# Maximum over the last axis of 64 MiB: larger and fewer loads, a larger share for GpSimd, and VectorE's steps in a written order

## The chip, the cores and the metric

One core of one Trainium2 chip. The metric is the device time of one execution in microseconds (us); a kernel's time is the median of its executions. Each execution also has a **span**, from the first to the last instruction that the profiler records; the time is the span and some 1.8 us outside it. All runs of this study were in the fast state. VectorE is DVE in the profile, GpSimd is POOL, ScalarE is ACT, SyncE is SP, TensorE is PE (its weight loads PEld).

## The reference

```python
# x: float32 [32, 512, 1024], normally distributed
def reference(x):
    return np.max(x, axis=-1).astype(np.float32)
```

There are 16384 rows of 1024 numbers. Each of the 128 partitions gets 128 rows; below, "a row" is one row on every partition, 128 x 4 KiB. 64 MiB are read once and 64 KiB written.

## The kernel before

SyncE issues the loads into a ring of 46 rows. VectorE reduces most rows directly. For some late rows GpSimd helps with the first few blocks of 128 columns: TensorE transposes a block, ScalarE copies it from PSUM, GpSimd takes the maximum over the partitions, TensorE transposes the result back into a column ("back"), and VectorE merges it with what it reduced itself. The last two rows come in three pieces. Cuts are marked with `# ...`.

```python
BLOCKS = [
    [15, 15, 15, 14, 12, 11, 9, 8, 7, 6],
    [4, 3, 2, 2, 1, 1, 1],
]
RING = 46
SHARED = {7: (2, 3), 9: (4, 4), 11: (3, 3), 13: (2, 3), 16: (1, 1)}   # load: (rows, blocks of 128 columns)
# ...
    for sizes in BLOCKS:
        S = sum(sizes) + 2 * (sizes is BLOCKS[-1])
        xb = xf[first * P:(first + S) * P, :].rearrange("(p i) d -> p i d", p=P)   # S rows per partition
# ...
    def turn(j, c):                      # one chunk: transposes, copy, all-reduce
        # ...
                in_turn("PE", nc.tensor.transpose(
                    out=ps[:, k * P:(k + 1) * P],
                    in_=rows(j)[:, loads[j][1] - m + r + i, c0 * P:(c0 + 1) * P],
                    identity=ident,
                ))
        in_turn("ACT", nc.scalar.copy(out=sb[:, :W], in_=ps[:, :W]))
        in_turn("POOL", nc.gpsimd.partition_all_reduce(
            top[:, :W], sb[:, :W], P, bass_isa.ReduceOp.max))
    def back(j, c):                      # one transpose for each block again
        # ...
                in_turn("PE", nc.tensor.transpose(
                    out=share(j)[:, c0, r + i:r + i + 1],
                    in_=tops[j, c][0:1, k * P:(k + 1) * P],
                    identity=ident[0:1, 0:1],
                ))
# ...
    for p, q in ((0, 48), (48, 96), (96, P)):
        store = nc.scalar.dma_start(out=views[0][0][p:q], in_=views[0][1][p:q])
    nc.scalar.dma_start(out=views[1][0], in_=views[1][1])
```

A point to keep in mind: the row numbers of a block are split so that partition p has S rows next to each other. Neighbouring partitions therefore read memory S x 4 KiB apart, here 448 KiB in the first block (112 rows) and 64 KiB in the second (16 rows).

## Time and profile before

| | before |
|---|---|
| time, median (range of 4 executions beside the changed kernel) | 164.03 us (163.90 to 164.27) |
| span of the profiled execution | 162.3 us |
| bytes loaded, mean rate over the span | 67.11 MB, 414 GB/s |
| VectorE busy | 135.4 us |
| GpSimd's all-reduces | 7, 16.0 us |
| TensorE transposes | 76, two instructions each |

The lines of the profile and how they are read are in the prediction below: the load queue is busy to the end, and VectorE's queue ends just behind it.

### The profile page before, as it was taken

Reading aid. Unit: us, or ns where it says so; the run is one execution under the profiler, and the core shown is the slowest. Engines: PE = TensorE matmul, PEld = TensorE weight load, DVE = VectorE, ACT = ScalarE, POOL = GpSimd, SP = SyncE. Lnnn points to the kernel's source line nnn. Section 1 sums busy time; section 2 is a strip of 40 time slices with the busy share of each in tenths; the row PEclk is TensorE's granted clock in tenths of the full one; section 3 lists DMA queues with packets and bytes.
Section 4 is the critical chain, followed back from the end, with each engine's and each line's share of the span. In section 5 each row is a group of like instructions: output and inputs, shape, how many; then the busy total and the mean of one; then the engine's idle time right before and its main releaser. Section 6 shows DMA issues by size and latency. Waiting matters only on the chain.

```text
span 162.3 us, 305 instructions
## 1 busy us (share of the span) xinstructions
PE 14.0 (9%) x76; PEld 12.0 (7%) x76; DVE 135.4 (83%) x35; ACT 6.3 (4%) x8; POOL 16.2 (10%) x11
## 2 busy tenths in 40 slices
PE   0000000000000000000000000000003010736540
PEld 0000000000000000000000000000002010725440
DVE  3000079995999779998999999999999999999994
ACT  3000000000000000000000000000001000222020
POOL 0000000000000000000000000000000500095970
DMA  7999699988999699999998998999999999999990
GB/s 242 485 485 454 273 485 485 485 379 348 485 485 485 285 410 452 452 452 388 497 472 371 433 455 355 436 436 420 509 396 445 452 395 396 440 411 423 405 379 18
DMA packets 3200, 67.18 MB, mean 414 GB/s; under 512 B 640, under 2 KB 640, under 8 KB 1408
## 3 DMA queue, kind: packets, MB, share of 16 engines
q1 hardware_dynamic: 2880, 67.11, 96.7%
q10 hardware_dynamic: 320, 0.07, 0.2%
HBM read 67.11 MB, written 0.07 MB: 414 GB/s over the span
## 4 chain that ended last, share of the span: by engine, by line
DVE 57%; DMA 36%; issue 5%; DVEq 0%
DVE res L168 52%; DMA ring<-in_x_dram 36%; DVE fetched L168 5%; DVEq L249 0%
## 5 line engine op out<-in xcount | busy, mean ns | idle before, releaser
L168 DVE TENSOR_REDUCE res<-ring 128x15 f32<-128x15360 f32 (+10 forms) x15 | 124.1, 8302 | 23.7 <-DMA ring<-in_x_dram 23.7
L143 POOL PARTITION_ALL_REDUCE top<-sb x7 | 16.0, 2330 | 141.8 <-ACT sb L141 141.8
L135 PE MATMUL ps<-ident,ring 128*128 128x128 f32 x38 | 9.3, 425 | 133.8 <-DMA ring<-in_x_dram 133.8
L135 PEld LDWEIGHTS ps<-ident,ring 128*128 128x128 f32 x38 | 7.5, 223 | 134.1 <-issue 127.8
L141 ACT COPY sb<-ps 128x768 f32<-128x768 f32 (+3 forms) x7 | 5.1, 739 | 150.2 <-PE ps L135 150.2
L168 DVE TENSOR_REDUCE fetched<-ring 128x2 f32<-128x1280 f32 (+3 forms) x5 | 8.5, 1699 | 0.0
L161 PE MATMUL fetched<-ident,top 1*128 1x1 f32 x38 | 4.8, 243 | 10.8 <-DVE fetched L168 7.3
L161 PEld LDWEIGHTS fetched<-ident,top 1*128 1x128 f32 x38 | 4.5, 213 | 12.5 <-issue 8.0
L168 DVE TENSOR_REDUCE res<-res 128x2 f32<-128x672 f32 (+1 forms) x2 | 1.7, 858 | 0.0
L141 ACT ACT_TABLE_LOAD x1 | 1.3, 1283 | 0.7 <-PEq L238 0.7
L83 DVE MEMSET ident<- 128x128 f32 x1 | 0.2, 165 | 0.8 <-PEq L238 0.8
L168 DVE TENSOR_REDUCE res<-fetched 128x2 f32<-128x8 f32 (+3 forms) x5 | 0.7, 158 | 0.0
L90 DVE TENSOR_SCALAR rowno<-rowno 32x1 f32<-32x1 f32 x3 | 0.4, 146 | 0.1
L85 DVE TENSOR_TENSOR_SCAN colno<-ident 128x128 f32<-128x128 f32 x1 | 0.4, 425 | 0.0
L92 DVE TENSOR_SCALAR ident<-colno,rowno 128x128 f32<-128x128 f32 x1 | 0.3, 285 | 0.0
L87 DVE STREAM_TRANSPOSE rowno<-colno 128x32 f32<-128x32 f32 x1 | 0.2, 213 | 0.0
L238 POOL MEMSET const-float32-0.0<- 128x1 f32 x1 | 0.1, 98 | 0.2 <-issue 0.2
L238 POOL MEMSET const-bfloat16-1.0<- 128x1 bf16 x1 | 0.1, 101 | 0.0
L238 POOL MEMSET const-uint8-127<- 128x1 uint8 x1 | 0.1, 101 | 0.0
L238 POOL MEMSET const-float32-1.0<- 128x1 f32 x1 | 0.1, 99 | 0.0
L84 DVE MEMSET rowno<- 128x32 f32 x1 | 0.1, 85 | 0.0
## 6 DMA issues: line engine op xcount, KB each, us to landing
ring<-in_x_dram SPq DMA_DIRECT2D x3, 7680.0 KB, 38.4
ring<-in_x_dram SPq DMA_DIRECT2D x1, 7168.0 KB, 37.0
ring<-in_x_dram SPq DMA_DIRECT2D x1, 6144.0 KB, 33.4
ring<-in_x_dram SPq DMA_DIRECT2D x1, 5632.0 KB, 28.6
ring<-in_x_dram SPq DMA_DIRECT2D x1, 4608.0 KB, 39.1
ring<-in_x_dram SPq DMA_DIRECT2D x1, 4096.0 KB, 33.3
ring<-in_x_dram SPq DMA_DIRECT2D x1, 3584.0 KB, 29.0
ring<-in_x_dram SPq DMA_DIRECT2D x1, 3072.0 KB, 35.9
```

What stands on the lines that cost most here:

```text
L83: in_turn("DVE", nc.vector.memset(ident, 1.0))
L84: in_turn("DVE", nc.vector.memset(rowno, 0.0))
L85: in_turn("DVE", nc.vector.tensor_tensor_scan(out=colno, data0=ident, data1=ident, initial=-1.0, op0=ALU.add, op1=ALU.mult))
L87: in_turn("DVE", nc.vector.transpose(out=rowno, in_=colno[:, :32]))
L90: in_turn("DVE", nc.vector.tensor_scalar(out=part, in0=part, scalar1=float(q * 32), scalar2=None, op0=ALU.add))
L92: in_turn("DVE", nc.vector.tensor_scalar(out=ident, in0=colno, scalar1=rowno[:, 0:1], scalar2=None, op0=ALU.is_equal))
L135: in_turn("PE", nc.tensor.transpose(out=ps[:, k * P:(k + 1) * P], in_=rows(j)[:, loads[j][1] - m + r + i, c0 * P:(c0 + 1) * P], identity=i ...
L141: in_turn("ACT", nc.scalar.copy(out=sb[:, :W], in_=ps[:, :W]))
L143: in_turn("POOL", nc.gpsimd.partition_all_reduce(top[:, :W], sb[:, :W], P, bass_isa.ReduceOp.max))
L161: in_turn("PE", nc.tensor.transpose(out=share(j)[:, c0, r + i:r + i + 1], in_=tops[j, c][0:1, k * P:(k + 1) * P], identity=ident[0:1, 0:1],))
L168: return in_turn("DVE", nc.vector.reduce_max(out=out, in_=in_, axis=X))
L238: nc = _bacc.Bacc("TRN2", target_bir_lowering=False, num_devices=1)
```

## The change

Its intent: fewer loads (15 and three pieces instead of 17 and three), a ring fuller by one row, much more of the work for GpSimd (99 blocks instead of 38) and less for VectorE, and the steps of VectorE written in the order in which their inputs are expected. The result moves into the ring's tile. Cut to its core:

```diff
 BLOCKS = [
-    [15, 15, 15, 14, 12, 11, 9, 8, 7, 6],
-    [4, 3, 2, 2, 1, 1, 1],
+    [16, 15, 16, 15, 16, 15, 10, 7],
+    [5, 3, 3, 2, 1, 1, 1],
 ]
-RING = 46
-SHARED = {7: (2, 3), 9: (4, 4), 11: (3, 3), 13: (2, 3), 16: (1, 1)}
+RING = 47
+SHARED = {3: (4, 3), 5: (6, 5), 6: (10, 2), 7: (7, 1), 8: (3, 3), 9: (2, 4), 10: (2, 3), 11: (2, 3), 14: (1, 1)}
+PIECES = [(689, 335), (336, 688)]
+PLAN = """
+    d0 d1 d2 d3 t0 t1 b0 b1 p3 m3 d4 d5 t2 t3 t4 t5 b2 t6 b3 t7 b4 p5 b5 p6 t8 t9 t10 b6 b7
+    m5 p7 t11 b8 b9 b10 t12 m6 d8 t13 b11 p8 t14 m7 d9 b12 p9 b13 m8 d10 t15 p10 t16 p11 d12
+    b14 d13 b15 m9 m10 p14 t17 f0 b16 f1 b17 m11 m14 f2
+""".split()
@@
-    ring = once.tile([P, RING, D], F32)
-    res = once.tile([P, MID + D - W], F32)
+    ring = once.tile([P, I + RING * D], F32)
+    res = ring[:, :I]
@@
+    for step in PLAN:
+        issue()                       # each load whose slot has no reader left
+        kind, k = step[0], int(step[1:])
+        if kind in "dp":              # d: direct rows, p: the rest of shared rows
+            (direct if kind == "d" else partial)(k)
+            readers[k] -= 1
+        elif kind == "t":             # t: transposes, copy, all-reduce of a chunk
+            turn(k)
+            readers[chunks[k][0]] -= 1
+        elif kind == "b":             # b: a chunk's transposes back
+            back(k)
+        elif kind == "m":             # m: merge on VectorE
+            merge(k)
+        else:                         # f: the three pieces
+            inst = maximum(*tail[k])
# ... (the old loops and lists that this replaces are cut)
```

It also moves the border between the two blocks from row 112 to row 110, which at first looks like book-keeping: neighbouring partitions now read 440 and 72 KiB apart, and the last store writes 18 numbers (72 B) for each partition instead of 16 (64 B).

> **What bounds the kernel now.** I began with the page's engine shares, slices and queues.
>
> ```profile
> PE 14.0 (9%) x76; PEld 12.0 (7%) x76; DVE 135.4 (83%) x35; ACT 6.3 (4%) x8; POOL 16.2 (10%) x11
> ...
> DVE  3000079995999779998999999999999999999994
> ...
> q1 hardware_dynamic: 2880, 67.11, 96.7%
> ...
> DVE res L168 52%; DMA ring<-in_x_dram 36%; DVE fetched L168 5%; DVEq L249 0%
> ...
> res<-in_x_dram SPq DMA_DIRECT2D x1, 344.0 KB, 11.5
> ```
>
> The load queue is busy for 96.7% of the span. VectorE (DVE) is at 83%, but its low digits are all in the first 19 slices; the chain names both. To see which of the two sets the end I read VectorE's timeline, first and last part.
>
> ```profile
> 21.42 16.15 DVE L168 TENSOR_REDUCE res<-ring 128x15 f32<-128x15360 f32 x1 [18.91 <-DMA ring<-in_x_dram]
> 39.55 16.15 DVE L168 TENSOR_REDUCE res<-ring 128x15 f32<-128x15360 f32 x1 [1.98 <-DMA ring<-in_x_dram]
> ...
> 74.64 55.86 DVE L168 TENSOR_REDUCE res<-ring 128x14 f32<-128x14336 f32 x5 [0.79 <-DMA ring<-in_x_dram]
> ...
> 139.41 2.27 DVE L168 TENSOR_REDUCE res<-ring 128x2 f32<-128x2048 f32 x1
> ...
> 157.34 0.86 DVE L168 TENSOR_REDUCE res<-ring 128x1 f32<-128x689 f32 x1
> 158.24 0.85 DVE L168 TENSOR_REDUCE res<-res 128x2 f32<-128x672 f32 x1
> 159.01 0.22 DVE L168 TENSOR_REDUCE res<-fetched 128x2 f32<-128x8 f32 x2
> 159.15 0.86 DVE L168 TENSOR_REDUCE res<-res 128x1 f32<-128x689 f32 x1
> ```
>
> From 74.64 us on VectorE has no idle gap. Yet its end is no later than the data allow: the last piece is issued at 147.52 (below) and lands 11.5 us later (last line of the first fence), at 159.0, and its reduction starts at 159.15. So the kernel is **balanced**: the load stream ends at 159.0 and VectorE's queue ends within 0.15 us of it. Then come 0.86 us of reduction, the last store (1.4 us) and the close, to a span of 162.3; the timed median, 163.97, is 1.67 above the span.
>
> The stream's rate follows from the queue's timeline. From the ninth load on, an issue waits for the load eight places earlier, so these starts mark the landings of the loads of 7, 6, 4 and 3 rows:
>
> ```profile
> 131.63 0.33 SPq L185 DMA_DIRECT2D ring<-in_x_dram  x1
> 138.93 0.33 SPq L204 DMA_DIRECT2D ring<-in_x_dram  x1
> 143.82 0.33 SPq L206 DMA_DIRECT2D res<-in_x_dram  x1
> 147.52 0.33 SPq L207 DMA_DIRECT2D res<-in_x_dram  x1
> ```
>
> Six rows took 7.30 us, four 4.89, three 3.70, and fifteen 39.55 - 21.42 = 18.13. From 15 and 4: (18.13 - 4.89)/11 = 1.204 us for a row and **0.07 us for each load** besides. Six rows give 7.29: the stream never starves.
>
> [...] A row of 128 x 4 KiB in 1.204 us is 435.5 GB/s[...]. [...] From 16.15 us for 15 rows and 2.27 for 2 a row costs 1.067 us (0.96 elements per ns) and an instruction about 0.14, of which some 0.08 lie under its neighbour. [...] Two rows take 2.27 us at 139.41 with GpSimd idle and 2.28 at 150.23 with it busy[...]. This matters, since GpSimd will work far longer.
>
> **The change, part by part.**
>
> *Fewer loads.* 17 whole loads become 15 (16, 15, 16, 15, 16, 15, 10, 7, 5, 3, 3, 2, 1, 1, 1), with the same three pieces. Same bytes, two times 0.07 us less: the last piece lands at 159.0 - 0.14 = 158.85. For that the queue must never run dry. A ring of 47 rows holds 16+15+16. By the rule above the loads land at 22.6, 40.7, 60.1, 78.2, 97.6, 115.7, 127.8, 136.3, 142.4, 146.1, 149.8, 152.3, 153.5, 154.8 and 156.1. The nearest thing to a late issue is the load of 7, which waits for VectorE to finish the fifth load (97.6 + 17.2 = 114.8) and is due at 127.8. Hidden, with 13 us to spare.
>
> *Less work for VectorE.* GpSimd takes 38 blocks of 128x128 before and, counted from the list (12+30+20+7+9+8+6+6+1), 99 after. 61 blocks are 61/8 rows x 1.067 = 8.1 us less reduction. But the new work is beside loads that come in fatter and later pieces, so it shows as idle time in front of loads 0 to 4, not at the end. What counts is VectorE's queue after its last wait for data. I laid it out with the durations above: it is idle for some 0.3 us before the load of 7 (136.3), then has 18.4 row-equivalents up to the last whole load, 1.33 more in two pieces, in 13 instructions, and seven merges at about 0.08: 19.7 x 1.067 + 13 x 0.065 + 0.6 = 22.4 us, plus some 0.2 for waits on its own last write. The third piece's reduction can start at 136.3 + 22.6 = 158.9 to 159.0. The data are there at 158.85. So again both ends meet: **159.0 against 159.15, 0.15 us won.** Both starts of the chain (first load one row larger, 1.2 us later) cost nothing, as the stream does not wait for VectorE.
>
> *More for TensorE, ScalarE, GpSimd.* The seven all-reduces show
>
> ```profile
> 142.07 3.22 POOL L143 PARTITION_ALL_REDUCE top<-sb  x1 [13.89 <-ACT sb L141]
> ...
> 150.13 2.50 POOL L143 PARTITION_ALL_REDUCE top<-sb  x1 [1.64 <-ACT sb L141]
> ```
>
> for 8 and 6 blocks: about 0.34 us a block and 0.5 fixed. 18 of them with 99 blocks: 18 x 0.5 + 99 x 0.34 = 43 us, all between 115.7 and 158 save two early ones: GpSimd becomes nearly full there. With transposes at 0.21 us a block, copies of 0.16 + 0.10 a block and returns at 0.107 a block, I stepped through the four engines with the waits of the built program. Each merge on VectorE must find its returns done: 142.2 against 142.9 for the load of 10, 145.4 against 147.3 for that of 7, 149.4 against 149.7 for that of 5, 154.6 and 155.4 against 156.0 for the next two, 158.1 and 158.3 against 158.85 for the last two. All in time, two of them by less than 0.7 us.
>
> *Order of steps and the tail.* The pieces now land in the ring and need the load of 10 read (about 136); they are due at 156. The stores are as before.
>
> The sum: -0.15 us, 163.97 to 163.8. As every margin errs on one side, I take 163.9.
>
> **The rivals.** *GpSimd becomes the bound.* For: margins of 0.3 and 0.7 us, and one chain of four engines with two buffers each. Against: the trace's durations repeat to 3%. With all-reduces 6% longer my layout loses 0.15 us, at 10% 1.0 us, at 20% 4 us (168.0). *The stream's rate changes.* Rows of 64 KiB per partition (16 rows) have not run in this trace; 48 rows are loaded so, and 1% in their rate is 0.6 us either way. The partition pitch in memory goes from 448 to 440 KiB and from 64 to 72 KiB. Nothing shows a dependence: the 4-row load of the second block has the same cost per row as the first. *VectorE was the true bound, and 8 us less work gives a gain.* Against: the last piece's landing at 159.0 forbids more than 0.15 us. *A load is issued late* by a wait the scheduler added: the waits that I read name only the readers of the slots overwritten.
>
> **Range and chances.** The stream's end is certain to some 0.2 us if rates hold; slips of GpSimd add 0 to 1. I take 163.4 to 164.8. A 2% gain (160.7) would need the stream 3 us shorter[...]: 0.01. A 2% loss (167.2) needs GpSimd 18% slower or a starved queue: 0.02.
>
> **What would show it.** Right: VectorE idle before each of loads 0 to 5, hardly after 136; spacing of 19.3 us for 16 rows; POOL near 42 us busy; the last reduction starting near 159.0. Wrong: VectorE idle with a TensorE or GpSimd releaser before a merge (first rival); 16-row spacing off 19.3 (second); a gap in the queue's busy share after slice 5 (fourth).

## The result

The changed kernel takes **165.73 us** (165.44 to 165.84, 4 executions) against 164.03: a ratio of 1.0100 (95% interval 1.0088 to 1.0113). A ratio here is the record's, over the fast runs of both kernels, so not quite the ratio of the quoted medians. The record notes no wrong result. The profiled execution has a span of 163.5 us, against 162.3; the four executions have 2.14 to 2.24 us outside the span, where the kernel before had 1.7 to 1.8. So of 1.7 us, 1.2 are inside the span and **about 0.4 outside it**.

The changed kernel's page, the lines that answer to the first fence of the prediction (engines; queues; chain):

```profile
PE 34.9 (21%) x198; PEld 30.1 (18%) x198; DVE 128.0 (78%) x40; ACT 14.6 (9%) x19; POOL 41.8 (26%) x22
...
q1 hardware_dynamic: 2592, 67.11, 95.8%
...
q8 instruction: 1, 0.02, 0.0%
...
DMA ring<-in_x_dram 70%; DVE ring L74 23%; DVE got L74 2%; SPq L215 1%; DVEq L269 0%
```

The share of the load queue fell though it carries the same bytes. And there is a queue that the kernel before does not have: q8, one transfer of 0.02 MB of kind "instruction". The page calls its share 0.0%, which is the share of sixteen engines' span; it says nothing of what one of the sixteen was doing for others. VectorE's timeline of the changed kernel (start, duration, engine, line, operation; in brackets the idle time before and what ended it):

```profile
22.91 17.22 DVE L74 TENSOR_REDUCE ring<-ring 128x16 f32<-128x16384 f32 x1 [20.39 <-DMA ring<-in_x_dram]
41.02 16.15 DVE L74 TENSOR_REDUCE ring<-ring 128x15 f32<-128x15360 f32 x1 [0.90 <-DMA ring<-in_x_dram]
60.37 17.22 DVE L74 TENSOR_REDUCE ring<-ring 128x16 f32<-128x16384 f32 x1 [3.20 <-DMA ring<-in_x_dram]
...
116.02 9.75 DVE L74 TENSOR_REDUCE ring<-ring 128x9 f32<-128x9216 f32 x1 [0.93 <-DMA ring<-in_x_dram]
...
137.58 6.70 DVE L74 TENSOR_REDUCE got<-ring 128x7 f32<-128x6272 f32 x1 [1.19 <-DMA ring<-in_x_dram]
...
158.42 1.75 DVE L74 TENSOR_REDUCE ring<-ring 128x1 f32<-128x689 f32 x2
160.09 0.22 DVE L74 TENSOR_REDUCE ring<-got 128x2 f32<-128x8 f32 x2
160.23 0.86 DVE L74 TENSOR_REDUCE ring<-ring 128x1 f32<-128x689 f32 x1
```

The spacing of the landings is as foreseen (19.35 us for 16 rows: 60.37 - 41.02), but two of them are late. The first load lands at 22.9 instead of 22.6. The load of 7 rows lands at 137.56 instead of 136.3; from there all is late by about 1.1 us, and the last reduction starts at 160.23 instead of 159.0.

Was VectorE held up by GpSimd's chain, the first rival? The view of who waited for whom, the lines for VectorE in the changed kernel:

```profile
DVE ring L74 <- DMA ring<-in_x_dram: 30.9, 6, 20.4
...
DVE got L74 <- DMA ring<-in_x_dram: 1.2, 1, 1.2
```

Apart from 0.8 us at its first instruction, VectorE waited for loads only. No merge was late.

In the traces each load has 16 landings, and the page counts 16 DMA engines; I take each landing for the part of one engine, and what one engine moves for the load queue is called a DMA ring below (not the ring of rows that holds the data). In the kernel before, the first load's last ring is 0.51 us behind its first (20.88 to 21.39) and stays so to the end. In the changed kernel this spread is 0.90 us at the first load (21.98 to 22.88), 0.85 at the load of 10 rows, and then **1.79 at the load of 7** (135.77 to 137.56), which holds to the last whole load (1.78). The other fifteen land the load of 7 by 136.63, within 0.86 us: one ring lost time between 128.1 and 137.6 and never made it up. The q8 transfer lies in just that stretch: 16,384 B, from 132.41 us, for 1.03 us; the trace's only packet of the load of 7 that is long (1.56 us instead of 1.06) begins at 133.43, as the transfer ends (132.41 + 1.03). The trace doesn't name the ring of a packet, so that both used one ring is read from these times; the five traces with a fetch show it six times, to within 0.02 us. The reduction waits for the slowest ring: that lands at 137.56, and the reduction starts at 137.58.

### The profile page after: what moved, and what is told of

Same layout as the page of the kernel before. It is cut to its first block, busy times and chain, and to the rows that moved or that the text cites. A ratio compares the mean times of both kernels' runs of the same rounds, so it can differ in the third digit from the quotient of the medians.

```text
span 163.5 us, 606 instructions
## 1 busy us (share of the span) xinstructions
PE 34.9 (21%) x198; PEld 30.1 (18%) x198; DVE 128.0 (78%) x40; ACT 14.6 (9%) x19; POOL 41.8 (26%) x22
## 4 chain that ended last, share of the span: by engine, by line
DMA 70%; DVE 25%; issue 1%; SPq 1%; DVEq 0%
DMA ring<-in_x_dram 70%; DVE ring L74 23%; DVE got L74 2%; SPq L215 1%; DVEq L269 0%
## 5 line engine op out<-in xcount | busy, mean ns | idle before, releaser
L74 DVE TENSOR_REDUCE ring<-ring 128x1 f32<-128x1024 f32 (+7 forms) x14 | 99.1, 7082 | 30.9 <-DMA ring<-in_x_dram 30.9
L146 POOL PARTITION_ALL_REDUCE top<-sb x18 | 41.6, 2371 | 117.5 <-ACT sb L144 114.3
L138 PE MATMUL ps<-ident,ring 128*128 128x128 f32 x99 | 22.7, 410 | 114.3 <-DMA ring<-in_x_dram 113.0
L138 PEld LDWEIGHTS ps<-ident,ring 128*128 128x128 f32 x99 | 18.6, 216 | 115.5 <-DVE ring L74 78.6
L74 DVE TENSOR_REDUCE got<-ring 128x2 f32<-128x1280 f32 (+7 forms) x9 | 27.5, 3072 | 1.2 <-DMA ring<-in_x_dram 1.2
L144 ACT COPY sb<-ps 128x640 f32<-128x640 f32 (+6 forms) x18 | 13.3, 746 | 143.0 <-PE ps L138 127.3
L156 PE MATMUL got<-ident,top 1*128 1x1 f32 x99 | 12.7, 240 | 10.6 <-POOL top L146 7.5
L156 PEld LDWEIGHTS got<-ident,top 1*128 1x128 f32 x99 | 11.4, 206 | 14.2 <-POOL top L146 9.5
L74 DVE TENSOR_REDUCE ring<-got 128x2 f32<-128x8 f32 (+7 forms) x9 | 1.3, 165 | 0.0
```

The lines of the kernel that those rows point to most:

```text
L74: return in_turn("DVE", nc.vector.reduce_max(out=out, in_=in_, axis=X))
L138: in_turn("PE", nc.tensor.transpose(out=ps[:, w:w + P], in_=rows(j)[:, loads[j][1] - m + r + i, c * P:(c + 1) * P], identity=ident,))
L146: in_turn("POOL", nc.gpsimd.partition_all_reduce(top[:, :W], sb[:, :W], P, bass_isa.ReduceOp.max))
L156: in_turn("PE", nc.tensor.transpose(out=share(j)[:, c, r + i:r + i + 1], in_=tops[k][0:1, w:w + P], identity=ident[0:1, 0:1],))
```

## The experiments

Theory **F**: TensorE's program has 423 instructions instead of 173; the q8 transfer of kind "instruction" (16,384 B, 1.03 us) fetches a part of it while the kernel runs, and this fetch holds one ring. Rival **R**: loads of 64 KiB a partition are slow. Rival **G**: GpSimd's chain. Later theories: **P** (spacing of the partitions in memory), and **A**, **B**, **D** (length of ScalarE's, GpSimd's, VectorE's program) for what lies outside the span. "Instructions of an engine" are those in its compiled program; the traces hold three or four fewer of each engine. The experiments ran in three batches of four kernels, each batch on one chip; the kernel before took 164.04, 164.11 and 164.09 us on the three chips.

### 1. The changed kernel with few TensorE instructions: after_few_tensore

Each chunk transposes one block and the copy repeats it; each row sends one block back. 55 transposes instead of 198; everything else, waits included, stays, but for merges that read fewer columns. The result is wrong on purpose.

```diff
-        for i in range(q):
-            for c in range(parts):
+        for i in range(1):
+            for c in range(1):
                 # transposes of turn(); in back(): for c in range(1), and merge reads that block only
-        nc.scalar.copy(out=sb[:, :W], in_=ps[:, :W])
+        nc.scalar.copy(out=sb[:, :W].rearrange("p (k w) -> p k w", w=P),
+                       in_=ps[:, :P].unsqueeze(1).broadcast_to([P, W // P, P]))
```

> The changed kernel with the same loads, the same VectorE, ScalarE and GpSimd work and the same waits, but 55 TensorE transposes in place of 198 (each chunk transposes one block, the copy repeats it; wrong result on purpose). Theory F (the instruction fetch of 16 KB in the middle of the stream holds one of the 16 DMA rings for 1.03 us, and every later load waits for that ring): no fetch record in the span, the load of 7 rows lands near 136.5 instead of 137.56, time 164.0 to 164.6. Rival R (the 16-row loads of 64 KiB a partition slow the stream): the time stays within 0.3 us of 165.7. Rival G (VectorE waits for GpSimd's chain): the time stays too, since GpSimd's 18 all-reduces are all still there.

Measured: 165.43 us (5 executions, ratio 1.0079, interval 1.0067 to 1.0092), spans 162.9 to 163.3. The fetch is gone from the queues and the jump at the load of 7 with it: it lands at 136.75.

```profile
q1 hardware_dynamic: 2592, 67.11, 95.9%
q10 hardware_dynamic: 320, 0.07, 0.2%
```

**But the time hardly moved.** Theory F did not give its 164.0 to 164.6; by the time alone, this is what rivals R and G had expected. Three lines of two views of this run, VectorE's first and last reduction and the landing of the last store, say why:

```profile
23.03 17.22 DVE L74 TENSOR_REDUCE ring<-ring 128x16 f32<-128x16384 f32 x1 [20.52 <-DMA ring<-in_x_dram]
...
159.42 0.86 DVE L74 TENSOR_REDUCE ring<-ring 128x1 f32<-128x689 f32 x1
```

```profile
out_dram<-ring ACTq DMA_DIRECT2D x1, 9.0 KB, 2.0
```

The last reduction is 0.8 us earlier than in the changed kernel, so the fetch is real. Yet the first load's rings are 1.00 us apart (22.00 to 23.00), the last store takes 2.0 us to land (1.5 in the changed kernel, 1.4 before), and 2.2 us are outside the span as in the changed kernel. More than one thing is at work.

### 2. The kernel before with idle transposes: before_idle_transposes

```diff
+    ps = psum.tile([P, D], F32)
+    for k in range(122):
+        in_turn("PE", nc.tensor.transpose(
+            out=ps[:, k % 8 * P:k % 8 * P + P], in_=ident, identity=ident))
     loads = []
```

> The kernel before with 122 extra transposes of the identity right after it is made (us 2.5 to about 29, when TensorE has nothing else to do; nobody reads them), so that TensorE has 198 transposes as in the changed kernel. Theory F: a 16 KB instruction fetch appears in the span near 20 to 30 us, all later loads land about 1.0 us later than in the kernel before, time 165.0 to 165.8. Rivals R and G: nothing they name is changed, 164.0 within 0.2.

Measured: 165.42 us (4 executions, ratio 1.0082, 1.0068 to 1.0096), correct, span of the profiled execution 163.4. Its queues, and VectorE's first and last reduction:

```profile
q8 instruction: 1, 0.02, 0.0%
```

```profile
22.51 16.15 DVE L173 TENSOR_REDUCE res<-ring 128x15 f32<-128x15360 f32 x1 [19.99 <-DMA ring<-in_x_dram]
...
160.27 0.86 DVE L173 TENSOR_REDUCE res<-res 128x1 f32<-128x689 f32 x1
```

The fetch is at 16.09 us for 0.93 us, earlier than the 20 to 30 us expected. Fifteen rings land the first load between 20.75 and 21.40, the sixteenth at 22.49. Everything after is 1.1 us late: 160.27 against 159.15. It isn't TensorE's work as such that slows the loads: fifteen rings are on time. Idle work on an idle engine cost 0.8% of the time. **Theory F holds for the cost of a fetch**; 1.8 us outside the span show that TensorE's program is not what adds there.

### 3. The kernel before with a first load of 16 rows: before_first16

```diff
-    [15, 15, 15, 14, 12, 11, 9, 8, 7, 6],
+    [16, 15, 15, 14, 12, 11, 9, 8, 7, 5],
```

> The kernel before with its first load 16 rows instead of 15 (and the tenth 5 instead of 6). Rival R: the first load lands near 22.9 (0.3 us later than 21.39 + 1.21 = 22.60) and all later landings are 0.3 late, time 164.4 or more. If 64 KiB rows are harmless (theory F): first landing 22.6, last landing as before at 159.0, time within 0.2 of 164.15 (my ledger has VectorE's queue end 0.13 later through the larger first load).

Measured: 164.09 us (4 executions, ratio 1.0001), first landing 22.62, spread 0.53 us. **Rival R falls.**

### 4. The changed kernel without the share of the fourth load: after_without_share3

```diff
-SHARED = {3: (4, 3), 5: (6, 5), ...
-    d0 d1 d2 d3 t0 t1 b0 b1 p3 m3 d4 d5 t2 ...
+SHARED = {5: (6, 5), ...
+    d0 d1 d2 d3 d4 d5 t0 ...        (the later chunks renumbered)
```

> The changed kernel without GpSimd's share of the fourth load (4 rows, 12 blocks; VectorE takes them in time it is idle in front of the fifth load): 174 TensorE transposes instead of 198, correct result. Theory F, with the fetch tied to how many TensorE instructions have gone by: the fetch record moves from 132.4 to about 135 to 143 us, but is still in the stream and still costs 1 us: 165.3 to 165.8; if instead the shorter program needs no fetch: 164.0 to 164.6. Theory G: unchanged 165.7, as the late GpSimd work is the same.

Measured: 165.75 us (165.43 to 166.91, 4 executions; ratio 1.0116), spans 163.7 to 165.1, only 1.8 us outside. The fetch comes at 141.36 us, when 97 transposes had begun; in the changed kernel 90 had, in run 2 it was 102. So it goes with the number of TensorE instructions (187 to 207 of the trace's had started) and not with the time. The number is not sharp: run 9 has 93 transposes, and run 12, whose TensorE work is that of run 2 up to there, 121. In the profiled, slowest execution the fetch hit the ring that was last already: the spread went from 1.52 us at the first load to 3.03. Here the two losses add on one ring; in the changed kernel the spread went from 0.85 to 1.79 us only, as the fetch hit another ring than the last, and the larger loss covers the smaller. What the smaller time outside the span means came with run 11. Rival G, too, had expected this time (165.7); it falls by the waits of the changed kernel above, and by run 5, where all 18 all-reduces remain and the last reduction still starts at 158.84.

### 5 and 6. The spacing in memory, both ways: few_tensore_old_addresses, before_new_addresses

The kernel of run 1 reads with the spacing of the kernel before, and the kernel before with that of the changed one. Sizes and engines stay; both results are wrong on purpose.

```diff
-        xb = xf[first * P:(first + S) * P, :].rearrange("(p i) d -> p i d", p=P)
+        step, row = ((112, 0), (16, 14080))[sizes is BLOCKS[-1]]     # run 5; run 6: (110, 0), (18, 14078)
+        xb = bass.AP(tensor=xf.tensor, offset=xf.offset + row * D,
+                     ap=[[step * D, P], [D, S], [1, D]])
```

> The kernel of after_few_tensore (no instruction fetch in the span) with one more change: a partition's rows start 448 KiB apart in memory as in the kernel before (16 rows apart in the last block), instead of 440 and 72 KiB; sizes, order and engines as they were (wrong result on purpose). Open is why the slowest ring ends the first load 1.0 us after the fastest there (0.5 in the kernel before), which all later loads keep. Theory P (the spacing in memory delays the first packets of a ring): spread of the first landing back to about 0.5 us, span 162.4 to 162.8 instead of 163.2. Rival T (the start is unlike for another reason: the ring shifted by 512 B, or what runs before the span): spread stays near 0.9 or more, span 162.9 to 163.3. The 2.2 us outside the span stay in both.

> The kernel before with the changed kernel's spacing in memory (110 and 18 rows between partitions, wrong result on purpose) and nothing else. Theory P: spread of the first landing 0.9 to 1.5 us, span 162.7 to 163.1, time 164.4 to 164.8. Rival T: 0.5 us, span 162.3, time 164.0 to 164.1.

Measured: run 5 takes 164.80 us (4 executions, 164.69 to 164.83), spans 162.5 to 162.6, against 165.43 of run 1 on another chip. Run 6 takes 164.46 (ratio 1.0020, interval 1.0005 to 1.0035), spans 162.5 to 162.9. VectorE's first and last reduction, of run 5 and then of run 6:

```profile
22.46 17.22 DVE L74 TENSOR_REDUCE ring<-ring 128x16 f32<-128x16384 f32 x1 [19.95 <-DMA ring<-in_x_dram]
...
158.84 0.86 DVE L74 TENSOR_REDUCE ring<-ring 128x1 f32<-128x689 f32 x1
```

```profile
21.65 16.15 DVE L170 TENSOR_REDUCE res<-ring 128x15 f32<-128x15360 f32 x1 [19.14 <-DMA ring<-in_x_dram]
...
159.38 0.86 DVE L170 TENSOR_REDUCE res<-res 128x1 f32<-128x689 f32 x1
```

With the old spacing the first load's rings are 0.37 us apart (1.00 in run 1), and the last reduction starts at 158.84, where the prediction's ledger had 158.9 to 159.0 and run 1 had 159.42. With the new spacing, the kernel before goes from 0.51 to 0.76 us and its last reduction is 0.23 late. **Theory P holds in both directions**, with 0.2 to 0.6 us, but run 6 is weak: its time was met (164.4 to 164.8), its spread was not (0.9 to 1.5 expected). The spread also varies without any change of spacing: in the eight traces with the old one and no fetch during the first load it is 0.36 to 0.66 us, in the four with the new one 0.76 to 1.52. The two don't overlap, but one trace for each kernel gives the size only roughly. What delays the rings is not seen. The whole spread is there when the first packets end (4.76 to 5.74 us in run 1, 4.79 to 5.19 in run 5): they begin up to 1.3 us apart in run 1, 0.35 in run 5, and take up to 3.7 and 3.3 us, where later packets of the same size take 2.42. From the second packet on all rings run alike.

No rate differs between the two spacings, only the start: at 440 KiB, in the changed kernel, 16 rows land in 19.35 us; the kernel before, at 448 KiB, has 1.204 us for a row and 0.07 for a load, which makes 19.33. The better spacing of the two is 448 KiB.

### 7 and 8. ScalarE's and GpSimd's program length: before_idle_copies, before_idle_memsets

```diff
+    scrap = once.tile([P, 1], F32)
+    for k in range(21):                                                  # run 7
+        in_turn("ACT", nc.scalar.copy(out=scrap, in_=colno[:, 0:1]))
+    for k in range(20):                                                  # run 8 has this instead
+        in_turn("POOL", nc.gpsimd.memset(scrap, 0.0))
```

> The kernel before with 21 ScalarE copies of one column at the start, so that ScalarE has 50 instructions as in the changed kernel (29 before). Open is the 0.42 us that the changed kernel (and after_few_tensore) take outside the span, 2.2 instead of 1.8, while after_without_share3 with 46 ScalarE and 48 GpSimd instructions takes 1.8. Theory A (the length of ScalarE's program): time minus span 2.2, time 164.4 to 164.5. Theory B (GpSimd's): 1.8, time 164.0 to 164.1.

> The kernel before with 20 GpSimd memsets of one column at the start, so that GpSimd has 50 instructions as in the changed kernel (30 before). Theory B (the length of GpSimd's program): time minus span 2.2, time 164.4 to 164.5. Theory A (ScalarE's): 1.8, time 164.0 to 164.1.

Measured: 164.09 and 163.97 us (2 executions each), 1.76 to 1.81 us outside the span in both. Neither A nor B.

### 9. The changed kernel, correct, with the old spacing: after_spacing448

```diff
-    [16, 15, 16, 15, 16, 15, 10, 7],
-    [5, 3, 3, 2, 1, 1, 1],
+    [16, 15, 16, 15, 16, 15, 10, 7, 2],
+    [3, 3, 3, 2, 1, 1, 1],          # and the later loads renumbered in SHARED and PLAN
```

> The changed kernel, correct, with its load of 5 rows cut into 2 and 3, so that the first block is 112 rows and the second 16 as in the kernel before: rows of neighbouring partitions lie 448 and 64 KiB apart instead of 440 and 72. Same steps on all engines, one load more (0.07 us), the fetch still there. Theory P (spacing in memory costs 0.3 to 0.6 us at the first load, and the last store of 18 columns some tenths): spread of the first landing 0.5 us, time 165.0 to 165.3. If spacing matters only in the kernels tried so far: 165.7 to 165.9.

Measured: 165.67 us (4 executions, ratio 1.0099, 1.0084 to 1.0114). A **miss**: 165.0 to 165.3 was expected. The spread of the first landing did go back to 0.53 us (first reduction below), and the last store back to 1.4 us, but the last reduction is no earlier:

```profile
22.48 17.22 DVE L72 TENSOR_REDUCE ring<-ring 128x16 f32<-128x16384 f32 x1 [19.97 <-DMA ring<-in_x_dram]
...
160.42 0.86 DVE L72 TENSOR_REDUCE ring<-ring 128x1 f32<-128x689 f32 x1
```

The fetch (132.57 us, 1.02 us) took the spread from 0.51 at the load of 10 rows to 1.98 at the load of 7. So a fetch cost its ring about **1.5 us** in these runs: the 1.0 of its own, and 0.5 by which the ring's next packet is longer (1.54 us instead of 1.06 here too). Run 4 shows it bare, on the ring that was last already: 1.49 to 3.03. My sum had added the fetch and the spacing; a landing takes the maximum over rings. In the changed kernel the fetch covers what the spacing costs.

### 10. The last store with 64 B a partition: few_tensore_store16

```diff
     # on top of run 5
-    nc.scalar.dma_start(out=views[1][0], in_=views[1][1])
+    nc.scalar.dma_start(
+        out=bass.AP(tensor=of.tensor, offset=of.offset + N - 16 * P, ap=[[16, P], [1, 16]]),
+        in_=res[:, I - 16:I])
```

> The kernel of few_tensore_old_addresses with its last store 16 columns wide (64 B a partition, as in the kernel before) instead of 18 (72 B). There the last store took 1.8 us to land, 2.0 in after_few_tensore, 1.4 in the kernel before. If the shape of the store is the reason: 1.4, span 162.1, time 164.3 to 164.4. If not: 1.8, span 162.5, time 164.8.

Measured: 164.45 us (4 executions, ratio 1.0022), spans 162.2 to 162.3; a part of the output is not written, on purpose. The last store, in run 5 and then here:

```profile
out_dram<-ring ACTq DMA_DIRECT2D x1, 9.0 KB, 1.8
```

```profile
out_dram<-ring ACTq DMA_DIRECT2D x1, 8.0 KB, 1.4
```

The store of 72 B a partition took 0.4 us longer in this pair. (The last reduction starts at 159.05 here, 0.2 later than in run 5 with the same loads: such is the spread between executions and chips.) In the changed kernel itself the store landed in 1.5, so there it accounts for about 0.1.

### 11. VectorE's program length: before_idle_vector

```diff
+    scrap = once.tile([P, 1], F32)
+    for k in range(9):
+        in_turn("DVE", nc.vector.memset(scrap, 0.0))
```

> The kernel before with 9 VectorE memsets of one column at the start, so that VectorE has 59 instructions as in the changed kernel (50 before, 57 in after_without_share3). ScalarE's and GpSimd's program lengths were tried and did nothing to the 0.42 us outside the span. Theory D (VectorE's program length passes a limit between 57 and 59): time minus span 2.2, time 164.4 to 164.5. If not: 1.8, 164.0 to 164.1, and the 0.42 us stay open.

Measured: 164.51 us (2 executions, 164.49 and 164.53; ratio 1.0028, 1.0008 to 1.0048), span 162.3 as in the kernel before, and **2.18 and 2.23 us outside**. Theory D. Nine instructions that end in the first four microseconds, long before the first load lands, make the execution 0.42 us longer, outside of what the profile shows. 57 instructions do not (run 4), 59 do; in all traces here it is 1.7 to 1.8 us with 50 or 57 and 2.1 to 2.2 with 59. Which step of starting or closing the program that is, no record shows.

### 12. Two fetches: before_idle250

The edit of run 2 with 250 in place of 122: 672 TensorE instructions.

> The kernel before with 250 idle transposes instead of 122 (672 TensorE instructions; 416 there, 173 in the kernel before). Theory F: a second fetch of 16 KB[...], on the same ring, so that the lag doubles: landings about 2 us later than in the kernel before, span 164.4 to 164.7, time 166.2 to 166.5. If the fetches go to different rings, the second hides behind the first: 165.3 to 165.6.

Measured: 165.50 us (2 executions), against 165.42 with one fetch. Queues, and VectorE's last reduction:

```profile
q8 instruction: 2, 0.03, 0.1%
```

```profile
160.50 0.86 DVE L173 TENSOR_REDUCE res<-res 128x1 f32<-128x689 f32 x1
```

The fetches are at 18.55 and 32.20 us. After the first, one ring lands 1.43 us behind the fifteenth; from the second load on **two** rings do (40.84 and 40.87, the other fourteen between 38.99 and 39.40). The second hides behind the first, as the expectation's alternative had it.

### The sum

| kernel | fetch in the stream | spacing (KiB) | last store | VectorE instructions | time (us) | outside the span |
|---|---|---|---|---|---|---|
| before | no | 448, 64 | 64 B | 50 | 164.03 to 164.11 | 1.7 to 1.8 |
| before_new_addresses | no | 440, 72 | 64 B | 50 | 164.46 | 1.8 |
| before_idle_vector | no | 448, 64 | 64 B | 59 | 164.51 | 2.2 |
| before_idle_transposes | yes | 448, 64 | 64 B | 50 | 165.42 | 1.8 |
| few_tensore_store16 | no | 448, 64 | 64 B | 59 | 164.45 | 2.2 |
| few_tensore_old_addresses | no | 448, 64 | 72 B | 59 | 164.80 | 2.2 |
| after_few_tensore | no | 440, 72 | 72 B | 59 | 165.43 | 2.2 |
| after_without_share3 | yes | 440, 72 | 72 B | 57 | 165.75 | 1.8 |
| after_spacing448 | yes | 448, 64 | 64 B | 59 | 165.67 | 2.2 |
| after | yes | 440, 72 | 72 B | 59 | 165.73 | 2.2 |

The row few_tensore_store16 is the change without its three side effects inside the span: it is slower than the kernel before by 0.36 us, and all of this is the 0.42 outside. So the new sizes, shares and order are worth what was predicted for them (0.15) at most, and no measured version beats the kernel before. One that keeps the new sizes, needs no fetch and is correct was not run: a fetch came after 90 to 121 transposes in each of the five kernels here that have more (174 to 326), and GpSimd's share alone needs 198.

## Why the prediction was wrong

The prediction was 163.9, range 163.4 to 164.8, with chances of 0.01 and 0.02 for a gain or a loss of 2%. The change did stay within 2%, but 165.73 lies outside the range, and the sign of the forecast 0.15 us is wrong. None of the four rivals named is what happened.

- **"Fewer loads ... the last piece lands at 159.0 - 0.14 = 158.85. For that the queue must never run dry."** This is the step that failed. The queue did not run dry; one of its sixteen rings did other work. The ledger treated the load queue as one server with a rate, and its end as "certain to some 0.2 us if rates hold". The rates held. The load of 7 was as late as its slowest ring (137.56, where the others had landed by 136.63), and a transfer from outside the kernel's own list put one ring 1.5 us back: 0.9 us more spread at the load of 7. VectorE's idle time in front of that load, foreseen as 0.3 us, was 1.19; with its own queue of 22.6 us behind it, the end moved by as much. Without fetch and with the old spacing (run 5) the idle time was 0.28 and the last reduction started at 158.84, so the term was right for what it counted.
- **"Nothing shows a dependence" on the spacing.** The kernel before has one spacing in its first block, and the start of the stream happens once; the last block's equal cost per row could not show it. The dependence sits in the first packets, and is worth 0.2 to 0.6 us when no fetch covers it (runs 1, 5 and 6).
- **"The timed median ... is 1.67 above the span"** was carried over as a constant. It grew by 0.42 us with VectorE's program (run 11).
- **"VectorE's queue after its last wait", 22.6 us:** right. From the start of the load of 7's reduction to that of the last it was 160.23 - 137.58 = 22.65 us.
- **"More for TensorE, ScalarE, GpSimd":** GpSimd's all-reduces (41.6 us, 43 foreseen) and the merges, all in time, were right, so the first rival fell. But TensorE's part was counted in time (198 transposes, nearly all hidden) and not in instructions. Here the cost of hidden work on an idle engine was in its program.
- **Rows of 64 KiB:** harmless (run 3), as assumed.

The sum, worked out again with what the runs show: last reduction at 159.0 foreseen, 1.2 later through the fetch, about 0.1 for the close with the wider store, 0.4 outside: 163.8 + 1.7 = 165.5, against 165.73 measured. The remaining 0.2 is no larger than the spread between executions and chips.

What the traces show of the fetches is a count: one transfer of 16,384 B each; none with 173 TensorE instructions, one with 375 to 423, two with 672. The prediction rested on the profile of the kernel before, which has none.

## What to carry to other kernels

When loads fill every DMA ring to the end, count what else will use a ring, instructions included (here one fetch of 16,384 B put its ring about 1.5 us back): compare the length of each engine's program with the one you replace, and look in the profile for a queue of kind "instruction". Moving work to an idle engine need not be free there, even when its time is hidden: 122 idle transposes cost 1.4 us in run 2. And treat a change of the row split as a change of addresses: test it alone, because a ring that started late here stayed late (in the kernel before the last ring is 0.51 us behind the first at the first load, 0.49 at the last whole one).

## What the runs show of the hardware, in numbers

- In run 2 TensorE did not wait for the fetch (its 122 idle transposes, 15.9 us busy, show no idle time but the 2.6 us before the first; the fetch, at 16.09 us, lies among them), but the loads did: 1.0 us for the transfer and 0.5 us in the next packet on that ring, and the kernel before became 1.4 us longer (164.04 to 165.42) through 122 idle transposes. A second fetch on another ring (run 12) added under 0.1 us (165.50).
- The first fetch was seen when 90 to 121 transposes (two instructions each) had begun.
- A step of 0.42 us outside the span came between 57 and 59 VectorE instructions (1.8 to 2.2 us); its cause is open.
- The spacing in memory changed the first packets only: rings 0.36 to 0.66 us apart at 448 KiB, 0.76 to 1.52 us at 440 KiB; after that 16 rows took 19.35 us at 440 KiB, against 19.33 worked out from the rows at 448.
- A row of 512 KiB took 1.204 us in the kernel before, which is 435 GB/s; in the changed kernel (19.35 - 0.07)/16 = 1.205 us.
- A last store of 128 x 72 B took 1.5 us to land in the changed kernel, 1.8 in run 5 and 2.0 in run 1; one of 128 x 64 B took 1.4 us in the kernel before, in run 10 and in six more.
